# A gated attention, pooling and ConvFFN layer on one core: first q weights on ScalarE's queue, k's heads copied ahead of pooled tiles, the second norm's squares on ScalarE and its sums inside the first up tiles

## The chip, the core and the metric

The kernel runs on one core of one Trainium2 chip. The metric is the device time of one execution in microseconds (us). Three timed executions of the kernel before are given, and one further execution was profiled. Engines are named as in the profile: PE is TensorE's matmul (PEld its weight load), DVE is VectorE, ACT is ScalarE, POOL is GpSimd, SP is SyncE, and a name with q behind it (SPq) is that engine's instruction issue.

## The reference

One decoder layer over 256 tokens of width 1024, in float32:

```python
h = rmsnorm(x, norm_mix_g)
q, k, v, u_pool, gate_logits = split(h @ w_in)         # 512, 512, 512, 512, 2048
q, k = rotary(rmsnorm(heads(q))), rotary(rmsnorm(heads(k)))
attn = causal_softmax_attention(q, k, heads(v))        # 8 heads of 64; one block of 256, so plain causal
pooled = multiscale_pool_mixer(u_pool, w_pool, pool_scale)
gates = sigmoid(gate_logits + b_gate)
x = x + (gates[0] * (attn @ w_branch_attn) + gates[1] * (pooled @ w_branch_pool)) @ w_out
h2 = rmsnorm(x, norm_ffn_g)
gate, val = split(causal_depthwise_conv(h2 @ w_up, conv_w, conv_b))   # 2 x 2816 columns
return x + (silu(gate) * val) @ w_down
```

## The kernel before, in words

Everything is kept transposed, features on the 128 partitions and the 256 tokens along the free axis. Each float32 operand is split into a rounded high part (`high`, line 80, a copy on ACT) and a rest (`low`, lines 84 and 86, a subtraction on DVE), and `mm3` (lines 92 to 94) adds three matmuls: high by high, high by low, low by high. So each weight chunk of 1 MB (128 x 2048) needs two ACT copies (`hi_...`) and two DVE subtractions (`lo_...`) of 128 x 1024 before PE may use it. The calls of `ahead()` that are strewn through the program emit these pieces some chunks before their use, and the subtraction that ends a chunk lets SP issue the next weight transfer (`load`).

The stages follow each other: the start (x and q's weights come interleaved in the tensor `xq` by five transfers on SP's queue, lines 191 to 195, of 1, 1, 2, 2 and 2 of the eight contraction slices; eight small matmuls on `ones`, `ps_warm`, run on PE in the meantime); projections q, k, v (`project`, `ps_q`, `ps_k`, `ps_v`); four pool tiles (`ps_u`) and sixteen gate tiles (`ps_g`, the loop of line 497), among which attention is woven; the two branches (`ps_bp`, `ps_ba`); the output projection (`ps_out`, eight tiles, each followed by `residual`); then 44 up tiles (`ps_up`) and 22 down steps (`ps_d`); at the end eight output transfers on SP's queue (line 700).

The order on every engine is the order in which the program is written, and each engine runs its instructions in that order. The parts that the change touches:

- Line 189 is a first tiny activation on ACT, which makes ACT load its function table. Line 194 issues the `xq` transfers.
- `to_heads` (line 310) transposes a normed q or k tile on PE into a PSUM bank (`ps_tq`, `ps_tk`) and copies it on ACT to `qkT`. For k it is called at the head of iteration n = 1 (`KREADY`), behind what `tick()` and `ahead()` of iteration 0 put on ACT: a copy of a pooled tile (`poolh`, line 400) and a high part (`hi_g`). `scores` (line 426) at n = 2 multiplies q and k (`ps_s`).
- `residual` (line 566) runs once per output tile j: DVE adds the tile to x (`xq`, line 567), ACT makes the high part of the scaled x (`hhi`), POOL squares x (`ss`, `s`, lines 571 and 574) and adds the square to the sum `ss2` (line 575), `ahead()` puts an ACT copy and a DVE subtraction of a weight piece in between, and DVE makes the rest (`hlo`, line 577).
- `token_rms` (line 235) sums `ss2` over the partitions by two tiny matmuls (`ps_n`, line 238), DVE scales the result (`var_n`, line 240), POOL takes it to the power -0.5 (`rtok`, line 241). `diagonal` (line 243) puts `rtok` on a diagonal on DVE (`diag`), `spread_rms` (line 247) spreads it over all partitions by a matmul (`ps_n`, line 249) and copies it to `R2`. Every up tile is multiplied by `R2` when it leaves PSUM (line 606).
- Lines 649 to 664 are the first up tiles: both tiles of chunk 0 over seven of eight contraction slices, then their last slice, then the sums, then six slices of the next tile, then the spread.

Of the kernel before, what the change touches and what calls it, by code (L numbers as in the profile page):

```python
# [10 lines left out]
AF = mybir.ActivationFunctionType  # L11
ALU = mybir.AluOpType
AX = mybir.AxisListType

P = 128
S = 256
NT = S // P
# [36 lines left out]
KREADY = 1  # L54
# [5 lines left out]
def hybrid_layer_kernel(ctx: ExitStack, tc: tile.TileContext, xq_d, par_d, wkv_d, wpg_d,  # L60
# [128 lines left out]
    nc.scalar.activation(scrap, ones[:, 0:1], AF.Copy)  # L189

    cut = 0
    for k in XCUTS:
        end = KD + k * (S + AW)
        nc.sync.dma_start(out=xq_all[:, cut:end], in_=xq_d[:, cut:end])
        cut = end
    load(2)
# [300 lines left out]
    for n in range(2 * KD):  # L497
        if n == KREADY:
            for t in range(NT):
                to_heads(kg[t], t, kT, "k")  # L500
        if n >= FIRST and (n - FIRST) % 4 == 0:
            scores((n - FIRST) // 4)
        if n == 10:
            pool_maps()
            ahead()
        b, c = n // 2, n % 2
        if c == 0:
            w = chunk("g")
        ps = feature_tile(w, c, f"g{n}")
        tick()  # L510
        ahead(AHEAD if n % 2 else 0)
        nc.vector.tensor_tensor(gate(n), ps[:, 0:S], R1, ALU.mult)
        if n >= 2 * KD - 2:
            sigmoids(3)
# [51 lines left out]
    def residual(j, ps):  # L566
        nc.vector.tensor_tensor(xT[:, j, :], ps[:, 0:S], xT[:, j, :], ALU.add)
        g = par[:, C_FFN + j:C_FFN + j + 1]
        high(hhi[:, j, :], xT[:, j, :], g)
        if j == 0:  # L570
            nc.gpsimd.tensor_tensor(ss2, xT[:, j, :], xT[:, j, :], ALU.mult)
        else:
            s2 = tmp.tile([P, S], F32, tag="s2", name=f"s2_{j}")
            nc.gpsimd.tensor_tensor(s2, xT[:, j, :], xT[:, j, :], ALU.mult)
            nc.gpsimd.tensor_tensor(ss2, ss2, s2, ALU.add)
        ahead(AHEAD if j % 2 == 0 else 0)
        low(hlo[:, j, :], hhi[:, j, :], xT[:, j, :], g)
# [73 lines left out]
    for ks in (range(KD - 1), range(KD - 1, KD)):  # L651
        for c in range(2):
            tile_part(w0, (hhi, hlo), c, ps0[c], ks)
    ahead()
    ahead()
    stat = ps2.tile([P, 2, 512], F32, tag="ps2", name="ps_n2")
    token_rms(stat[:, 0, :], ss2, rtok2, "n2")
    ahead()
    w = chunk("up")
    ps = [bank("ps_up1_0")]  # L660
    tile_part(w, (hhi, hlo), 0, ps[0], range(6))
    diagonal(rtok2)
    spread_rms(stat[:, 1, 0:S], R2)
    tile_part(w, (hhi, hlo), 0, ps[0], range(6, KD))
# [30 lines left out]
    for m in (0, 2, 4, 6, 1, 3, 5, 7):  # L695
# [4 lines left out]
        nc.sync.dma_start(out=out_d[:, m, :], in_=xT[:, m, :])  # L700
# [73 lines left out]
```

## Time and profile before

| what | us |
|---|---|
| median of three timed executions | 350.35 |
| the three | 350.35, 350.55, 348.51 |
| the profiled execution, whole | 348.69 |
| its span | 346.9 |
| PE busy in the span | 340.7 (98%) |
| DVE, ACT, POOL busy | 261.0, 195.7, 101.5 |

The span is the stretch that the profiler shows, from the first instruction to the last; the profiled execution is 1.8 us longer than its span. PE's busy time counts pipelined matmuls with modelled ends: two matmuls that follow each other at full pace overlap in the records, so a stall of PE is read from the distance between starts, not from gaps of the busy time. A row of the timeline has start, duration, engine, line, operation, output and inputs, shapes, count, and in brackets how long the engine was idle before and who ended that.

### The profile page before, as it was taken

To read this page: it belongs to the slowest core of one execution; us is meant where nothing else is said; L and a number is where in the kernel's file an instruction comes from. 1 tells how busy PE (TensorE), PEld (TensorE's weight loads), DVE (VectorE), ACT (ScalarE), POOL (GpSimd) and SP (SyncE) were. 2 spreads that over 40 slices of the span, in tenths; PEclk is the share of its full clock that TensorE was granted. 3 is DMA by queue.
4 is the path that set the end of the run, shared out by engine and by line. 5 is a ranking of instruction groups with operands and counts; after the bars stand their busy time and mean duration, and the time that the engine had idled before them with its cause. 6 is when DMAs were issued, how large, how long until landed. Compare 5 with 4: busy or idle time off the path is not lost.

```text
span 346.9 us, 6715 instructions
## 1 busy us (share of the span) xinstructions
PE 340.7 (98%) x2736; PEld 329.2 (95%) x2736; DVE 261.0 (75%) x411; ACT 195.7 (56%) x311; POOL 101.5 (29%) x111
## 2 busy tenths in 40 slices
PE   8999999999999999999999999999999999999996
PEld 6887899999899999999999999999999999999995
DVE  4969889787587585899699877776777777777643
ACT  4956534634748945665367655555555555646420
POOL 1007991112202034586232212121212121212230
PEclk9999999999999999999999999999999999999999
DMA  7985642465272651566257555464636363652003
GB/s 275 419 327 213 222 159 110 150 220 213 69 259 92 242 201 45 175 237 211 109 168 271 188 224 201 164 222 145 242 123 243 131 235 132 232 162 83 0 2 121
DMA packets 10254, 62.76 MB, mean 181 GB/s; under 512 B 1136, under 2 KB 2288, under 8 KB 3312
## 3 DMA queue, kind: packets, MB, share of 16 engines
q1 hardware_dynamic: 10224, 62.34, 49.5%
q8 instruction: 21, 0.34, 0.4%
q14 instruction: 9, 0.07, 0.1%
HBM read 61.29 MB, written 1.05 MB: 180 GB/s over the span
## 4 chain that ended last, share of the span: by engine, by line
PE 80%; DVE 10%; DMA 4%; ACT 2%; issue 2%; SPq 1%; POOL 0%; ACTq 0%
PE ps_up L93 11%; PE ps_up L94 11%; PE ps_up L92 11%; PE ps_d L636 6%; PE ps_d L637 6%; PE ps_d L635 6%; PE ps_g L92 4%; PE ps_g L94 4%; PE ps_g L93 4%; DMA raw_k<-in_wkv 4%; PE ps_v L278 3%; DVE lo_up L84 2%; DVE hlo L86 2%; PE ps_bp L92 1%; PE ps_ba L94 1%
## 5 line engine op out<-in xcount | busy, mean ns | idle before, releaser
L92 PE MATMUL ps_up<-hhi,hi_up 128*128 128x256 f32 x352 | 98.5, 280 | 0.0
L93 PE MATMUL ps_up<-hlo,hi_up 128*128 128x256 f32 x352 | 98.4, 279 | 0.1
L94 PE MATMUL ps_up<-hhi,lo_up 128*128 128x256 f32 x352 | 98.3, 279 | 0.0
L93 PEld LDWEIGHTS ps_up<-hlo,hi_up 128*128 128x128 f32 x352 | 66.2, 188 | 0.4 <-DVE hlo L86 0.4
L92 PEld LDWEIGHTS ps_up<-hhi,hi_up 128*128 128x128 f32 x352 | 66.2, 188 | 0.0
L94 PEld LDWEIGHTS ps_up<-hhi,lo_up 128*128 128x128 f32 x352 | 66.2, 188 | 0.0
L84 DVE TENSOR_TENSOR lo_up<-raw_up,hi_up 128x1024 fp32r<-128x1024 f32 x44 | 55.9, 1273 | 6.1 <-ACT hi_up L80 6.1
L618 POOL TENSOR_TENSOR c_v<-c_g,c_v 128x256 f32<-128x256 f32 x22 | 16.2, 738 | 120.8 <-DVE c_v L601 120.8
L636 PE MATMUL ps_d<-al,hi_dn 128*128 128x256 f32 x176 | 49.1, 279 | 0.0
L635 PE MATMUL ps_d<-ah,hi_dn 128*128 128x256 f32 x176 | 49.1, 279 | 0.0
L637 PE MATMUL ps_d<-ah,lo_dn 128*128 128x256 f32 x176 | 49.1, 279 | 0.0
L80 ACT ACTIVATE hi_up<-raw_up 128x1024 fp32r<-128x1024 f32 x44 | 44.9, 1045 | 0.0
L92 PE MATMUL ps_g<-xhi,hi_g 128*128 128x256 f32 x128 | 36.5, 285 | 0.0
L93 PE MATMUL ps_g<-xlo,hi_g 128*128 128x256 f32 x128 | 35.7, 279 | 0.0
L94 PE MATMUL ps_g<-xhi,lo_g 128*128 128x256 f32 x128 | 35.7, 279 | 0.0
L80 ACT ACTIVATE ah<-c_v 128x256 fp32r<-128x256 f32 x22 | 9.2, 418 | 45.8 <-POOL c_v L618 45.8
L637 PEld LDWEIGHTS ps_d<-ah,lo_dn 128*128 128x128 f32 x176 | 33.1, 188 | 0.0
L635 PEld LDWEIGHTS ps_d<-ah,hi_dn 128*128 128x128 f32 x176 | 33.1, 188 | 0.0
L636 PEld LDWEIGHTS ps_d<-al,hi_dn 128*128 128x128 f32 x176 | 33.1, 188 | 0.0
L606 DVE TENSOR_TENSOR u_v<-ps_up,R 128x256 f32<-128x256 f32 x22 | 9.3, 421 | 26.1 <-PE ps_up L94 26.1
L84 DVE TENSOR_TENSOR lo_dn<-raw_dn,hi_dn 128x1024 fp32r<-128x1024 f32 x22 | 27.8, 1264 | 0.4 <-ACT hi_dn L80 0.4
L642 POOL TENSOR_TENSOR al<-c_v,ah 128x256 fp32r<-128x256 f32 x22 | 23.0, 1045 | 11.6 <-ACT ah L80 11.6
(182 smaller groups left out, 815.8 us busy)
## 6 DMA issues: line engine op xcount, KB each, us to landing
raw_up<-in_wup SPq DMA_DIRECT2D x22, 1024.0 KB, 4.8
raw_dn<-in_wdn SPq DMA_DIRECT2D x11, 1024.0 KB, 4.8
raw_g<-in_wpg SPq DMA_DIRECT2D x8, 1024.0 KB, 4.8
raw_o<-in_wout SPq DMA_DIRECT2D x4, 1024.0 KB, 4.8
xq<-in_xq SPq DMA_DIRECT2D x3, 768.0 KB, 7.4
raw_v<-in_wkv SPq DMA_DIRECT2D x2, 1024.0 KB, 14.1
raw_p<-in_wpg SPq DMA_DIRECT2D x2, 1024.0 KB, 6.3
raw_bp<-in_wbp SPq DMA_DIRECT2D x2, 1024.0 KB, 4.8
```

Source lines behind the costliest of these rows:

```text
L80: nc.scalar.activation(hi, src, AF.Copy, scale=scale)
L84: nc.vector.tensor_tensor(lo, src, hi.bitcast(F32), ALU.subtract)
L92: nc.tensor.matmul(out, sh, mh, start=start, stop=False, **kw)
L93: nc.tensor.matmul(out, sh, ml, start=False, stop=False, **kw)
L94: nc.tensor.matmul(out, sl, mh, start=False, stop=stop, **kw)
L278: nc.tensor.matmul(pt[t], sx[:, k, t * P:(t + 1) * P], wx[:, sl], start=k == 0 and sx is xhi and wx is hi, stop=k == KD - 1 and wx is lo)
L606: nc.vector.tensor_tensor(u, ps[:, 0:S], R2, ALU.mult)
L618: nc.gpsimd.tensor_tensor(uc[1], g[1], uc[1], ALU.mult)
L635: nc.tensor.matmul(o, hi[:, sl], acch[i], start=first, stop=False, skip_group_check=True)
L636: nc.tensor.matmul(o, hi[:, sl], accl[i], start=False, stop=False, skip_group_check=True)
L637: nc.tensor.matmul(o, lo[:, sl], acch[i], start=False, stop=i == KF - 1, skip_group_check=True)
L642: nc.gpsimd.tensor_tensor(accl[i], act_i, acch[i].bitcast(F32), ALU.subtract)
```

## The change

The transfer of the first slice is cut in two: its 512 columns of q weights are issued by ACT, its 264 columns of x (with the norm's gains) by SP, and the tiny activation that loads ACT's table goes behind the loop. `KREADY` becomes 0, and the call of `to_heads` for k stands behind the first gate tile and ahead of `tick()`. In `residual` the eight squares go from POOL to ACT; the seven additions stay on POOL. The sums of `token_rms` go ahead of the last slice of chunk 0's tiles, the three calls of `ahead()` behind that slice, and the spread behind all eight slices of the next tile. The last of the eight output transfers is cut into two halves of 64 partitions, one on SP's queue, one on ACT's.

```diff
--- before.py
+++ after.py
@@ -51,7 +51,7 @@
 STAGGER = 1
 AHEAD = 4
 FFN_AHEAD = 6
-KREADY = 1
+KREADY = 0
 FIRST = 2
 XCUTS = (1, 2, 4, 6, 8)
 
@@ -186,13 +186,18 @@
     xlo = act.tile([P, KD, S], F32R, tag="xlo", name="xlo")
     par = const.tile([P, C_END], F32, name="par")
     scrap = const.tile([P, 1], F32, name="scrap")
-    nc.scalar.activation(scrap, ones[:, 0:1], AF.Copy)
 
     cut = 0
     for k in XCUTS:
         end = KD + k * (S + AW)
-        nc.sync.dma_start(out=xq_all[:, cut:end], in_=xq_d[:, cut:end])
+        if k == 1:
+
+            nc.scalar.dma_start(out=xq_all[:, KD + S:end], in_=xq_d[:, KD + S:end])
+            nc.sync.dma_start(out=xq_all[:, 0:KD + S], in_=xq_d[:, 0:KD + S])
+        else:
+            nc.sync.dma_start(out=xq_all[:, cut:end], in_=xq_d[:, cut:end])
         cut = end
+    nc.scalar.activation(scrap, ones[:, 0:1], AF.Copy)
     load(2)
     nc.sync.dma_start(out=par, in_=par_d)
     for _ in range(RAWBUFS - 1):
@@ -495,9 +500,6 @@
             low(pooll[:, g, :], poolh[:, g, :], o, par[:, C_PS + g:C_PS + g + 1])
 
     for n in range(2 * KD):
-        if n == KREADY:
-            for t in range(NT):
-                to_heads(kg[t], t, kT, "k")
         if n >= FIRST and (n - FIRST) % 4 == 0:
             scores((n - FIRST) // 4)
         if n == 10:
@@ -507,6 +509,9 @@
         if c == 0:
             w = chunk("g")
         ps = feature_tile(w, c, f"g{n}")
+        if n == KREADY:
+            for t in range(NT):
+                to_heads(kg[t], t, kT, "k")
         tick()
         ahead(AHEAD if n % 2 else 0)
         nc.vector.tensor_tensor(gate(n), ps[:, 0:S], R1, ALU.mult)
@@ -568,10 +573,10 @@
         g = par[:, C_FFN + j:C_FFN + j + 1]
         high(hhi[:, j, :], xT[:, j, :], g)
         if j == 0:
-            nc.gpsimd.tensor_tensor(ss2, xT[:, j, :], xT[:, j, :], ALU.mult)
+            nc.scalar.activation(ss2, xT[:, j, :], AF.Square)
         else:
             s2 = tmp.tile([P, S], F32, tag="s2", name=f"s2_{j}")
-            nc.gpsimd.tensor_tensor(s2, xT[:, j, :], xT[:, j, :], ALU.mult)
+            nc.scalar.activation(s2, xT[:, j, :], AF.Square)
             nc.gpsimd.tensor_tensor(ss2, ss2, s2, ALU.add)
         ahead(AHEAD if j % 2 == 0 else 0)
         low(hlo[:, j, :], hhi[:, j, :], xT[:, j, :], g)
@@ -648,20 +653,19 @@
 
     w0 = chunk("up")
     ps0 = [bank(f"ps_up0_{c}") for c in range(2)]
-    for ks in (range(KD - 1), range(KD - 1, KD)):
-        for c in range(2):
-            tile_part(w0, (hhi, hlo), c, ps0[c], ks)
-    ahead()
-    ahead()
+    for c in range(2):
+        tile_part(w0, (hhi, hlo), c, ps0[c], range(KD - 1))
     stat = ps2.tile([P, 2, 512], F32, tag="ps2", name="ps_n2")
     token_rms(stat[:, 0, :], ss2, rtok2, "n2")
-    ahead()
+    for c in range(2):
+        tile_part(w0, (hhi, hlo), c, ps0[c], range(KD - 1, KD))
+    for _ in range(3):
+        ahead()
     w = chunk("up")
     ps = [bank("ps_up1_0")]
-    tile_part(w, (hhi, hlo), 0, ps[0], range(6))
+    tile_part(w, (hhi, hlo), 0, ps[0], range(KD))
     diagonal(rtok2)
     spread_rms(stat[:, 1, 0:S], R2)
-    tile_part(w, (hhi, hlo), 0, ps[0], range(6, KD))
     ug = normed(ps0[0], 0, "g0")
     uv = normed(ps0[1], KF, "v0")
     gate_done(0, ug)
@@ -697,7 +701,10 @@
             down(i, (m,))
         o = acc[m // 2][:, (m % 2) * S:(m % 2 + 1) * S]
         nc.vector.tensor_tensor(xT[:, m, :], o, xT[:, m, :], ALU.add)
-        nc.sync.dma_start(out=out_d[:, m, :], in_=xT[:, m, :])
+        if m < 7:
+            nc.sync.dma_start(out=out_d[:, m, :], in_=xT[:, m, :])
+    for q, rows in ((nc.sync, slice(0, P // 2)), (nc.scalar, slice(P // 2, P))):
+        q.dma_start(out=out_d[rows, 7, :], in_=xT[rows, 7, :])
 
 
     last = {}
```

Three places where instructions stand otherwise. The first is ACT around the copies of k's heads (`qkT<-ps_tk`); `poolh<-pl` are copies of pooled tiles, `hi_g` high parts of gate weights. Before:

```order
L80 ACTIVATE poolh<-pl_600 128x256
L80 ACTIVATE hi_g_560<-raw_g_363 128x1024
L80 ACTIVATE poolh<-pl_647 128x256
L80 ACTIVATE hi_g_654<-raw_g_427 128x1024
L315 ACTIVATE qkT<-ps_tk_661 128x4x128
L315 ACTIVATE qkT<-ps_tk_667 128x4x128
L80 ACTIVATE poolh<-pl_698 128x256
```

And in the changed kernel:

```order
L80 ACTIVATE poolh<-pl_601 128x256
L80 ACTIVATE hi_g_561<-raw_g_364 128x1024
L320 ACTIVATE qkT<-ps_tk_648 128x4x128
L320 ACTIVATE qkT<-ps_tk_654 128x4x128
L80 ACTIVATE poolh<-pl_660 128x256
L80 ACTIVATE hi_g_667<-raw_g_428 128x1024
L80 ACTIVATE poolh<-pl_699 128x256
```

The two copies of k's heads have moved ahead of one pooled tile and one high part; PE's order does not change there.

The second place is PE in the first up tiles. `ps_up_0` and `ps_up_1` are the two tiles of chunk 0 (high part `hi_up_1713` before, `hi_up_1714` after), the third tile uses the next chunk, and `ps_n` are the sums. Before:

```order
L94 MATMUL ps_up_1_1893<-hhi,lo_up_1714 128x256
L92 MATMUL ps_up_0_1892<-hhi,hi_up_1713 128x256
L93 MATMUL ps_up_0_1892<-hlo,hi_up_1713 128x256
L94 MATMUL ps_up_0_1892<-hhi,lo_up_1714 128x256
L92 MATMUL ps_up_1_1893<-hhi,hi_up_1713 128x256
L93 MATMUL ps_up_1_1893<-hlo,hi_up_1713 128x256
L94 MATMUL ps_up_1_1893<-hhi,lo_up_1714 128x256
L238 MATMUL ps_n_1950<-ones,ss_1604 128x1 x2
L92 MATMUL ps_up_0_1956<-hhi,hi_up_1783 128x256
```

And in the changed kernel:

```order
L94 MATMUL ps_up_1_1894<-hhi,lo_up_1715 128x256
L243 MATMUL ps_n_1937<-ones,ss_1605 128x1 x2
L92 MATMUL ps_up_0_1893<-hhi,hi_up_1714 128x256
L93 MATMUL ps_up_0_1893<-hlo,hi_up_1714 128x256
L94 MATMUL ps_up_0_1893<-hhi,lo_up_1715 128x256
L92 MATMUL ps_up_1_1894<-hhi,hi_up_1714 128x256
L93 MATMUL ps_up_1_1894<-hlo,hi_up_1714 128x256
L94 MATMUL ps_up_1_1894<-hhi,lo_up_1715 128x256
L92 MATMUL ps_up_0_1957<-hhi,hi_up_1784 128x256
```

The sums have moved ahead of six matmuls. The spread stands 18 matmuls into the third tile before, and behind all 24 of it after.

The third place is DVE behind the last residual. `lo_up` of two numbers are pieces of two later chunks. Before:

```order
L86 SCALAR_TENSOR_TENSOR hlo<-xq,par,hhi 128x256
L84 TENSOR_TENSOR lo_up_1854<-raw_up_1677,hi_up_1853 128x1024
L84 TENSOR_TENSOR lo_up_1943<-raw_up_1717,hi_up_1942 128x1024
L240 TENSOR_SCALAR var_n_1953<-ps_n_1950 128x2
L245 TENSOR_SCALAR diag<-ident,rtok_165 128x128 x2
L250 COPY R_164<-ps_n_1950 128x256
```

And in the changed kernel:

```order
L86 SCALAR_TENSOR_TENSOR hlo<-xq,par,hhi 128x256
L245 TENSOR_SCALAR var_n_1940<-ps_n_1937 128x2
L84 TENSOR_TENSOR lo_up_1855<-raw_up_1678,hi_up_1854 128x1024
L84 TENSOR_TENSOR lo_up_1950<-raw_up_1718,hi_up_1949 128x1024
L250 TENSOR_SCALAR diag<-ident,rtok_166 128x128 x2
L255 COPY R_165<-ps_n_1937 128x256
```

`var_n` has moved ahead of two subtractions of 128 x 1024, which stand between it and `diag` now.

## Rows read from the trace of the kernel before

**Rows 1.** The page: busy time, share of the span and instructions of each engine; and the shares of the engines in the chain of work that ended last.
```profile
PE 340.7 (98%) x2736; PEld 329.2 (95%) x2736; DVE 261.0 (75%) x411; ACT 195.7 (56%) x311; POOL 101.5 (29%) x111
...
PE 80%; DVE 10%; DMA 4%; ACT 2%; issue 2%; SPq 1%; POOL 0%; ACTq 0%
```

**Rows 2.** The list of waits, three of PE's weight loads that the prediction speaks of: engine, tile and line that waited, what ended the wait, us in total, times, longest.
```profile
PEld ps_s L430 <- ACT qkT L315: 0.7, 1, 0.7
...
PEld ps_n L249 <- DVE diag L245: 0.6, 1, 0.6
...
PEld ps_up L93 <- DVE hlo L86: 0.4, 1, 0.4
```

**Rows 3.** The busy time of each engine in the stretch of the up and down stage: from and to, length, then for PE, PEld, DVE, ACT and POOL busy us and instructions, granted clock, DMA share, GB/s.
```profile
166.00:344.00 178.00, 177.62 (x1520) 177.37 (x1520) 130.74 (x200) 97.16 (x146) 39.22 (x44) 1.00 0.45 162
```

**Rows 4.** The timeline of the scores' place, ACT first, then PE.
```profile
53.90 1.04 ACT L80 ACTIVATE hi_g<-raw_g 128x1024 fp32r<-128x1024 f32 x1
57.88 0.42 ACT L80 ACTIVATE poolh<-pl 128x256 fp32r<-128x256 f32 x1 [2.94 <-DVE pl L399]
...
59.15 1.06 ACT L315 ACTIVATE qkT<-ps_tk 128x512 f32<-128x512 f32 x2
```
```profile
55.96 1.04 PE L314 MATMUL ps_tk<-ident,qg_k 128*128 128x128 f32 x8
...
59.52 0.27 PE L94 MATMUL ps_g<-xhi,lo_g 128*128 128x256 f32 x1
60.27 0.71 PE L430 MATMUL ps_s<-qkT 64*128 64x256 f32 x4 [0.47 <-ACT qkT L315]
```

**Rows 5.** The timeline of the second norm, PE alone.
```profile
158.76 0.28 PE L92 MATMUL ps_up<-hhi,hi_up 128*128 128x256 f32 x1
...
159.19 0.39 PE L93 MATMUL ps_up<-hlo,hi_up 128*128 128x256 f32 x1
...
162.69 0.50 PE L238 MATMUL ps_n<-ones,ss 128*128 128x1 f32 x4
163.05 0.36 PE L92 MATMUL ps_up<-hhi,hi_up 128*128 128x256 f32 x1
...
165.12 0.28 PE L94 MATMUL ps_up<-hhi,lo_up 128*128 128x256 f32 x1
165.82 0.70 PE L249 MATMUL ps_n<-diag,ones 128*128 128x256 f32 x2 [0.42 <-DVE diag L245]
```

**Rows 6.** The same stage on DVE: a wait for a high part at the first residual, then the last residual and what follows it.
```profile
141.66 1.23 DVE L84 TENSOR_TENSOR lo_o<-raw_o,hi_o 128x1024 fp32r<-128x1024 f32 x1 [0.39 <-ACT hi_o L80]
...
156.62 0.41 DVE L567 TENSOR_TENSOR xq<-ps_out,xq 128x256 f32<-128x256 f32 x1
...
159.06 0.41 DVE L567 TENSOR_TENSOR xq<-ps_out,xq 128x256 f32<-128x256 f32 x1
159.39 1.42 DVE L84 TENSOR_TENSOR lo_up<-raw_up,hi_up 128x1024 fp32r<-128x1024 f32 x1
160.74 0.83 DVE L86 SCALAR_TENSOR_TENSOR hlo<-xq,par,hhi 128x256 fp32r<-128x256 f32 x1
161.50 2.90 DVE L84 TENSOR_TENSOR lo_up<-raw_up,hi_up 128x1024 fp32r<-128x1024 f32 x2
164.32 0.15 DVE L240 TENSOR_SCALAR var_n<-ps_n 128x2 f32<-128x2 f32 x1
165.29 0.48 DVE L245 TENSOR_SCALAR diag<-ident,rtok 128x128 f32<-128x128 f32 x2 [0.82 <-POOL rtok L241]
```

**Rows 7.** The same stage on POOL, and the durations of the rests on DVE's line 86 (ns, least, median, most): the first norm's (`xlo`, while POOL is idle) and the second norm's (`hlo`).
```profile
159.70 1.59 POOL L574 TENSOR_TENSOR s<-xq 128x256 f32<-128x256 f32 x1
161.37 0.81 POOL L575 TENSOR_TENSOR ss<-ss,s 128x256 f32<-128x256 f32 x1
```
```profile
L86 DVE SCALAR_TENSOR_TENSOR xlo<-xq,xhi x8: 478/480/485, 4.8 to 13.3; 128x256 fp32r<-128x256 f32 x8
L86 DVE SCALAR_TENSOR_TENSOR hlo<-xq,par,hhi x8: 476/831/952, 142.8 to 160.7; 128x256 fp32r<-128x256 f32 x8
```

**Rows 8.** The timeline of the start.
```profile
0.74 2.40 SPq L194 DMA_DIRECT2D xq<-in_xq  x5
...
4.43 0.63 ACT L80 ACTIVATE hi_q<-xq 128x512 fp32r<-128x512 f32 x1 [2.20 <-DMA xq<-in_xq]
...
5.11 1.12 PE L278 MATMUL ps_q<-hi_q,xhi 128*128 128x512 f32 x2 [0.28 <-ACT hi_q L80]
...
7.65 0.51 ACT L80 ACTIVATE xhi<-xq 128x256 fp32r<-128x256 f32 x1 [0.87 <-DMA xq<-in_xq]
...
7.93 0.63 PE L278 MATMUL ps_q<-lo_q,xhi 128*128 128x512 f32 x2
...
8.73 0.74 PE L278 MATMUL ps_q<-hi_q,xhi 128*128 128x512 f32 x2 [0.17 <-ACT hi_q L80]
```

**Rows 9.** The list of DMA issues: tile and source, queue, count, KB each, us from issue to landing.
```profile
out_T<-xq SPq DMA_DIRECT2D x8, 128.0 KB, 1.9
xq<-in_xq SPq DMA_DIRECT2D x1, 388.0 KB, 3.7
...
raw_pool<-in_wpool SPq DMA_DIRECT2D x1, 256.0 KB, 2.6
```

**Rows 10.** The output transfers by their tile: durations of the issues in ns (least, median, most), first and last start.
```profile
L700 SPq DMA_DIRECT2D out_T<-xq x8: 332/332/348, 339.2 to 344.1; - x8
```

## The prediction

> **What bounds the kernel now.** I read the page first: PE is busy for 340.7 of 346.9 us, the others 75% and less, and 80% of the chain that ended last is PE, 10% DVE [rows 1]. So a change can win only where PE stands still. Then the pace: 1520 matmuls in the 178.00 us from 166 to 344, so 0.117 us from one start to the next, without a stall over all that stretch [rows 3]. About half of the kernel, and all that follows the second norm, is therefore fixed, and I looked for stalls only before it. The list of waits names three that the change aims at: scores on the copy of k's heads, up matmuls on `hlo`, the spread on `diag` [rows 2]. Their price I take from starts, less one pace: 60.27 - 59.52 - 0.117 = 0.63 us [rows 4]; 159.19 - 158.76 - 0.117 = 0.31 us and 165.82 - 165.12 - 0.117 = 0.58 us [rows 5]. Sum 1.52 us. The other two places, start and end, are no waits on an engine but on transfers.
>
> **Scores.** The transposes of k's heads end at 57.0 on PE, but ACT copies only from 59.15, behind a pooled tile that came late from DVE and a high part. ACT stood idle for 2.94 us before that pooled tile, from 54.94 to 57.88 [rows 4]. In the new order the copies find that hole: from about 57.0, two copies in 1.06 us, done by 58.1, while PE arrives at the scores at 59.64. The whole 0.63 us goes. The pooled tile, ready at 57.88, slips by 0.2 us, and the high part behind it too, which PE needs only some tiles later. Nothing is issued more or less. What is late next? From here PE's order is the same, and gate tiles need pieces that were made a chunk ahead; the list of waits has no further one of PE or its weight loads from there to the up tiles of over 0.3 us, so I carry the 0.63 us through, with 0.3 as the low end.
>
> **Squares from POOL to ACT.** POOL loses eight squares, of 1.59 us for the last [rows 7], and keeps seven additions of 0.81. ACT gains eight squares of 128 x 256. This kernel has none of that shape; the copy of a pooled tile of that shape takes 0.42 us [rows 4], so 8 x 0.42 = 3.4 us on ACT, some 0.33 each in a row. ACT waits for DVE in that stage, except that the first residual's subtraction waits already 0.39 us for its high part [rows 6]: there the square delays DVE by 0.33 us, and once more at the third residual, where two pieces are due again: 0.66 us against the change.
>
> For it speaks DVE's relief. DVE runs behind PE here: one residual takes 159.06 - 156.62 = 2.44 us, of which a subtraction of 1.42 and an `hlo` of 0.83 [rows 6], which without POOL beside it takes 0.48 [rows 7]. The last square began at 159.70 and ended at 161.29, across the end of the subtraction and the start of `hlo` at 160.74 [rows 6, 7]. After the change the addition stands there instead: ready about 1.3 us after the residual, so again at the end of the subtraction. So I leave `hlo` at 0.83 and give back only the subtraction's excess over a free one (1.23 in the first row of rows 6): 0.2 us a residual. Over six residuals 1.2 us, less the 0.66, leaves 0.5 us, and the wait for `hlo` needs 0.31. It goes, narrowly: credit 0.31, bounds 0 (the lag stays) and 0.31; below nothing in a rival.
>
> The Trainium skill ("SBUF — State Buffer", Who interferes with whom) says that VectorE with two SBUF inputs and GpSimd take turns on one shared port pair, whole instruction by whole instruction, the second one blocked until the first is through. The trace agrees that both are slowed, but 0.35 us of `hlo` is less than a whole POOL operation of 0.81. By the rule taken literally `hlo` would wait for a full addition; that is rival 3.
>
> **Sums earlier.** Call the start of the sums t. Before, PE goes on at t + 0.36, and `var_n` at 164.32 is held by two subtractions in front of it on DVE, so `diag` starts at 165.29 and PE stalls [rows 5, 6]. After, `var_n` runs when the sums are there, about t + 0.55 (0.50 for the sums [rows 5] and a little for the signal), POOL's power runs beside the two subtractions (2.90 us for the pair before, 2.3 to 2.9 now), and `diag` (0.48) ends between t + 3.5 and t + 4.1. PE reaches the spread at t + 0.36 + 30 x 0.117 = t + 3.87: six matmuls and a whole tile of 24. So the stall of 0.58 us falls to between 0 and 0.25; I take 0. The price is that DVE waits at `var_n` for PE: behind it stand the two subtractions and the load they release, for chunks that PE starts over 5 us later, which covers it. The sums themselves need the last addition: before, at 162.18 [rows 7]; now they are due at 156.66 + 42 x 0.117 = 161.6. With the square on ACT and no DVE lag the addition ends near 160; with the old lag it would end at 161.3 at the latest. `R` comes 0.3 us later relative to the tile, and a PSUM bank is needed only a tile (2.8 us) later: cost nothing.
>
> **Start.** The first matmul at 5.11 follows the landing at 4.43 and one ACT copy. But PE stands again before 8.73: 8.73 - 7.93 - 2 x 0.233 = 0.33 us (two matmuls of twice the columns, so of two paces each), since the third slice's transfer (x's `xhi` at 7.65 waited for it) is late [rows 8]. So a first matmul earlier by any amount gains nothing unless the third transfer is earlier as well, and one later by 0.33 us costs nothing. The bytes ahead of the third are the same. The issue on ACT (0.48 us, a fifth of SP's 2.40) and the table load behind it fall into ACT's 2.20 us of idleness. I take 0; bounds: a gain of 0.33 if both queues ramp up faster, a loss of 6.2 if q's weights land with the last of SP's `xq` transfers.
>
> **End.** The last transfer of 128 KB lands 1.9 us after its issue; 256 KB took 2.6, so half the size would be 0.35 us shorter if halves ran apart [rows 9]. Issues are 0.33 us each, on two queues side by side [rows 10]. I take 0, since the two halves together are the same bytes, and keep 0.35 gained to 0.1 lost as the range.
>
> The Trainium skill ("DMA: Bandwidth & Descriptors", Rules for kernel authors) speaks against both edits: two transfers to partition halves serialize on the same 16 engines, and issuing from several queues only saves issue time. All transfers here left from SP, so no row shows it. By the rule the end gains 0, without it 0.35.
>
> **Sum.** 0.63 + 0.31 + 0.58 = 1.52 us. The profiled execution of 348.69 would become 347.2. The three timed runs lie at 348.51 and around 350.45, so the profiled one belongs to their lower end; off the median, 350.35 - 1.5 = 348.8.
>
> **The rivals.** (1) Start or end give as well: 0.33 at the third slice and 0.35 at the end, sum 2.2 us: 348.1. For it: the first transfer of 388 KB took 3.7 us where 256 KB took 2.6 [rows 9]. Against: the same bytes. 14 in 100. (2) The stalls in the norm move instead of going: squares hold up ACT's high parts, DVE stays behind, PE waits as long for `hlo` or `diag`. Only 0.63 stays: 349.7. For it: the margins of 0.2 to 0.4 us above are thin. 15 in 100. (3) POOL's addition, now always ready as the subtraction ends, blocks `hlo` for its full 0.81 instead of 0.35: a residual takes 2.24 + 0.46 = 2.70 us, 0.26 more than before, over five residuals 1.3, with ACT's 0.66 some 2.0 late, in place of the 0.31: 0.63 + 0.58 - 1.7 = -0.5: 350.8. Against: PE's tile takes 2.8 us, so DVE would still keep up. 6 in 100. (4) The slower one: q's weights on ACT's queue share the engines with four transfers of SP and land with the third slice, at 7.65 instead of 4.43. PE starts 3.2 us later, 0.33 of it free: +2.9, net +1.4: 351.7. It decides from a landing at 4.43 + 0.33 + 1.52 = 6.3. Against: at equal shares they land when twice their bytes have moved, near 4.4. 5 in 100. The forecast has the remaining 60.
>
> **How the numbers follow.** The likeliest case is 348.8, by itself 346.9 (if the lower of the two groups of times is met, 348.51 - 1.52 = 347.0) to 349.4. The range reaches to 350.8 (rivals 2 and 3, and the upper group) and to 346.4 (rival 1 in the lower group). About 1% is what a measurement of this kernel tells from no change. Faster by over 1% means under 346.85: the forecast in the lowest runs (8 in 100) and half of rival 1 (7). Slower by over 1% means over 353.9: only rival 4 near its far end, 4 in 100. The rest, 81, lies within 1%.
>
> **What would show it.** Right: scores follow the gate tile at one pace, with ACT's copies near 57; no wait for `hlo`, and start distances of 0.117 through the first up tiles; `var_n` ahead of its subtractions, and a spread with under 0.25 us of stall; first matmul anywhere up to 5.4 with the one near 8.73 unmoved; the last transfer landing 1.9 us after its issue. Wrong: the wait for `hlo` longer than 0.4 us, `hlo` over 1.2 us, a first matmul after 5.5, or new stalls between 61 and 139 that eat the 0.63.

## The result, and the profile after

The changed kernel takes 347.80 us (median of 13 runs, 347.71 to 348.66), the kernel before 350.14 (13 runs, 348.40 to 350.59): a ratio of 0.9949, 95% interval 0.9934 to 0.9964. The forecast was 348.8 in a range of 346.4 to 350.8, so the time lies inside it and within 1% of before. The executions of both kernels fall into a lower and an upper group (before: 6 of 13 at 348.40 to 348.81, 7 at 350.14 to 350.59; after: 11 at 347.71 to 348.01, 2 at 348.5 to 348.7); what five profiled executions show of this stands in the last section, and where the text compares tenths it takes the lower group. Like for like the change is worth 0.9 us: the profiled executions have spans of 346.9 and 346.0, and the lower groups have medians of 348.6 and 347.8. Three single executions in the experiments took 560 to 1866 us; they count in the medians of runs 1, 4 and 7 and are in no ratio and no group.

The page: busy time and instructions of each engine, and the engines' shares of the chain that ended last.
```profile
PE 340.3 (98%) x2736; PEld 329.3 (95%) x2736; DVE 259.3 (75%) x411; ACT 198.1 (57%) x319; POOL 89.4 (26%) x103
...
PE 90%; DMA 5%; DVE 3%; ACT 1%; issue 0%; POOL 0%; SPq 0%; ACTq 0%
```
Eight squares have gone from POOL to ACT, and DVE's share of the chain has fallen from 10% to 3% [rows 1]: PE waits for DVE much less. The list of waits has one of a weight load that was not there before (engine, tile and line that waited, what ended the wait, us, times, longest):
```profile
PEld ps_up L94 <- DVE lo_up L84: 0.2, 1, 0.2
```
The three waits of [rows 2] are gone from the list.

**Scores.** The timeline of their place, ACT, then PE:
```profile
56.51 1.09 ACT L320 ACTIVATE qkT<-ps_tk 128x512 f32<-128x512 f32 x2 [1.65 <-PE ps_tk L319]
57.79 0.42 ACT L80 ACTIVATE poolh<-pl 128x256 fp32r<-128x256 f32 x1 [0.19 <-DVE pl L404]
```
```profile
59.44 0.27 PE L94 MATMUL ps_g<-xhi,lo_g 128*128 128x256 f32 x1
59.64 0.71 PE L435 MATMUL ps_s<-qkT 64*128 64x256 f32 x4
```
The copies stand in the hole ahead of the pooled tile and end at 57.6, and PE goes on without a wait. From the last gate matmul to the first of the scores it is 59.64 - 59.44 = 0.20 us, where [rows 4] have 60.27 - 59.52 = 0.75: the place became 0.55 us shorter. PE is here 0.08 us earlier already (59.44 against 59.52).

**Second norm.** PE, DVE and POOL, in that order:
```profile
160.94 0.50 PE L243 MATMUL ps_n<-ones,ss 128*128 128x1 f32 x4
...
164.77 0.28 PE L94 MATMUL ps_up<-hhi,lo_up 128*128 128x256 f32 x1
164.88 0.59 PE L254 MATMUL ps_n<-diag,ones 128*128 128x256 f32 x2
...
183.65 0.28 PE L93 MATMUL ps_up<-hlo,hi_up 128*128 128x256 f32 x1
183.95 0.39 PE L94 MATMUL ps_up<-hhi,lo_up 128*128 128x256 f32 x1
184.18 0.28 PE L92 MATMUL ps_up<-hhi,hi_up 128*128 128x256 f32 x1
```
```profile
141.35 1.22 DVE L84 TENSOR_TENSOR lo_o<-raw_o,hi_o 128x1024 fp32r<-128x1024 f32 x1 [0.70 <-ACT hi_o L80]
...
144.35 0.48 DVE L86 SCALAR_TENSOR_TENSOR hlo<-xq,par,hhi 128x256 fp32r<-128x256 f32 x1
...
155.61 0.41 DVE L572 TENSOR_TENSOR xq<-ps_out,xq 128x256 f32<-128x256 f32 x1
...
157.96 0.41 DVE L572 TENSOR_TENSOR xq<-ps_out,xq 128x256 f32<-128x256 f32 x1
158.29 1.21 DVE L84 TENSOR_TENSOR lo_up<-raw_up,hi_up 128x1024 fp32r<-128x1024 f32 x1
159.42 0.97 DVE L86 SCALAR_TENSOR_TENSOR hlo<-xq,par,hhi 128x256 fp32r<-128x256 f32 x1
161.47 0.16 DVE L245 TENSOR_SCALAR var_n<-ps_n 128x2 f32<-128x2 f32 x1 [1.08 <-PE ps_n L243]
161.55 2.35 DVE L84 TENSOR_TENSOR lo_up<-raw_up,hi_up 128x1024 fp32r<-128x1024 f32 x2
163.82 0.48 DVE L250 TENSOR_SCALAR diag<-ident,rtok 128x128 f32<-128x128 f32 x2
165.52 0.42 DVE L255 COPY R<-ps_n 128x256 f32<-128x256 f32 x1 [1.22 <-PE ps_n L254]
```
```profile
159.36 0.75 POOL L580 TENSOR_TENSOR ss<-ss,s 128x256 f32<-128x256 f32 x1 [1.61 <-ACT s L579]
161.71 1.62 POOL L246 TENSOR_TENSOR rtok<-var_n,mhalf 128x2 f32<-128x2 f32 x1 [1.60 <-DVE var_n L245]
```
PE no longer waits for `hlo`, and the spread follows its predecessor by one pace of 0.11 us; in [rows 5] it came 0.70 after. The last residuals take DVE 157.96 - 155.61 = 2.35 us each instead of 2.44 [rows 6]: the subtraction fell from 1.42 to 1.21, `hlo` rose from 0.83 to 0.97. But PE waits at 183.95 for a `lo_up`: 183.95 - 183.65 - 0.12 = 0.18, and the matmul behind it starts 0.23 later instead of 0.12, so this stop costs 0.29 us in all. The stop at `hlo` in the kernel before had the same form; this row follows the one at 159.19 in [rows 5]:
```profile
159.42 0.28 PE L94 MATMUL ps_up<-hhi,lo_up 128*128 128x256 f32 x1
```

**Start and end.** The timeline of the start:
```profile
0.74 0.39 SPq L196 DMA_DIRECT2D xq<-in_xq  x1
0.74 0.41 ACTq L195 DMA_DIRECT2D xq<-in_xq  x1
...
5.27 1.22 PE L283 MATMUL ps_q<-hi_q,xhi 128*128 128x512 f32 x2 [0.43 <-DVE xlo L86]
...
7.63 0.51 ACT L80 ACTIVATE xhi<-xq 128x256 fp32r<-128x256 f32 x1 [0.81 <-DMA xq<-in_xq]
```
The first matmul comes at 5.27 instead of 5.11; the third slice's copy is where it was, at 7.63 against 7.65 [rows 8]. The end, the issues of the two halves first, then their rows in the list of DMA issues (count, KB each, us from the start of the issue to landing):
```profile
342.68 0.55 SPq L707 DMA_DIRECT2D out_T<-xq  x1
342.68 0.56 ACTq L707 DMA_DIRECT2D out_T<-xq  x1
```
```profile
out_T<-xq SPq DMA_DIRECT2D x1, 64.0 KB, 2.2
out_T<-xq ACTq DMA_DIRECT2D x1, 64.0 KB, 2.5
```
Each half takes 0.55 us to issue, where a whole tile took 0.33 [rows 10], and 2.2 and 2.5 us to land, where a whole tile took 1.9 [rows 9]. The span ends 346.0 - 342.68 = 3.3 us after the start of the last issue; before it was 346.9 - 344.1 = 2.8.

**The ledger of the two spans**, from starts on PE. To the first up matmul: 156.66 before, 156.04 after, 0.62 gained, of which 0.08 is there ahead of the scores already. From there through the spread to the next steady matmul: 166.48 - 156.66 = 9.82 against 165.44 - 156.04 = 9.40, and since the spread now stands 6 matmuls (0.70 us) later, 8.70 like for like: 1.12 gained. From there to the last matmul: 343.35 - 166.48 = 176.87 against 341.91 - 165.44 + 0.70 = 177.17: 0.30 lost, which is the stop at 183.95. The end: 346.9 - 343.35 = 3.55 against 346.0 - 341.91 = 4.09, 0.54 lost. Together 0.62 + 1.12 - 0.30 - 0.54 = 0.90, which is the difference of the spans.

### The profile page after: what moved, and what is told of

Same layout as the page of the kernel before. It is cut to its first block, busy times and chain, and to the rows that moved or that the text cites. A ratio compares the mean times of both kernels' runs of the same rounds, so it can differ in the third digit from the quotient of the medians.

```text
span 346.0 us, 6726 instructions
## 1 busy us (share of the span) xinstructions
PE 340.3 (98%) x2736; PEld 329.3 (95%) x2736; DVE 259.3 (75%) x411; ACT 198.1 (57%) x319; POOL 89.4 (26%) x103
## 3 DMA queue, kind: packets, MB, share of 16 engines
HBM read 61.29 MB, written 1.05 MB: 180 GB/s over the span
## 4 chain that ended last, share of the span: by engine, by line
PE 90%; DMA 5%; DVE 3%; ACT 1%; issue 0%; POOL 0%; SPq 0%; ACTq 0%
PE ps_up L94 12%; PE ps_up L92 12%; PE ps_up L93 12%; PE ps_d L642 6%; PE ps_d L641 6%; PE ps_d L640 6%; PE ps_g L92 5%; PE ps_g L94 4%; PE ps_g L93 4%; DMA raw_k<-in_wkv 3%; PE ps_v L283 3%; PE ps_out L92 2%; PE ps_out L94 2%; PE ps_out L93 2%; PE ps_bp L92 1%; DMA xq<-in_xq 1%
## 5 line engine op out<-in xcount | busy, mean ns | idle before, releaser
L84 DVE TENSOR_TENSOR lo_up<-raw_up,hi_up 128x1024 fp32r<-128x1024 f32 x44 | 54.5, 1242 | 6.1 <-ACT hi_up L80 6.1
```

What stands on the lines that cost most here:

```text
L84: nc.vector.tensor_tensor(lo, src, hi.bitcast(F32), ALU.subtract)
```

## The experiments

The medians of the kernel before beside these runs were 348.71, 348.77 and 348.81 (32 to 35 runs each, lower group around 348.65). "Lower" is the median of a kernel's lower group, with the number of executions in it.

**1. The end undone.** The changed kernel with the last tile as one transfer on SP.
```diff
-        if m < 7:
-            nc.sync.dma_start(out=out_d[:, m, :], in_=xT[:, m, :])
-    for q, rows in ((nc.sync, slice(0, P // 2)), (nc.scalar, slice(P // 2, P))):
-        q.dma_start(out=out_d[rows, 7, :], in_=xT[rows, 7, :])
+        nc.sync.dma_start(out=out_d[:, m, :], in_=xT[:, m, :])
```


> The changed kernel with its last output transfer whole again, on SP's queue, so the end edit alone undone. In the changed kernel's trace the two halves took 0.55 us to issue side by side and landed 2.2 and 2.5 us after, where the whole took 0.33 and 1.9; PE ends its last matmul 1.42 us earlier than before, but the span is only 0.9 us shorter. Theory A (the end edit costs what the issue and the landing grew by): the time from the last issue to the span's end falls by about 0.5 us, and the time from 347.8 to about 347.2 to 347.3. Rival B (the end of the span is set by something else, the closing instructions): span and time stay within 0.15 us of the changed kernel, 347.7 to 347.9.

Measured: 347.22 median, ratio to before 0.9944 (0.9923 to 0.9964); lower 347.16 (6 of 8), against the changed kernel's 347.79 (11 of 13). That is theory A: the end of the change costs 0.6 us. This is the best version by its median, ahead of both kernels.

**2. The norm alone.** Before, with the squares on ACT and the sums inside the first up tiles.
```diff
-            nc.gpsimd.tensor_tensor(s2, xT[:, j, :], xT[:, j, :], ALU.mult)
+            nc.scalar.activation(s2, xT[:, j, :], AF.Square)
...
-    tile_part(w, (hhi, hlo), 0, ps[0], range(6))
+    tile_part(w, (hhi, hlo), 0, ps[0], range(KD))
     diagonal(rtok2)
     spread_rms(stat[:, 1, 0:S], R2)
-    tile_part(w, (hhi, hlo), 0, ps[0], range(6, KD))
```


> The kernel before with the second norm's edits alone (squares on ScalarE, sums inside the first up tiles, spread after the whole tile). Theory A (stalls add up): the waits on hlo and diag go, 0.31 + 0.58 = 0.89 us, the span is about 346.0 and the runs near the lower group of before (348.5) become 347.6. Rival B (the gain needs the scores' edit as well, or is given back in the up tiles): under 0.4 us. On the two groups of before's times (near 348.5 and near 350.3): theory C says the upper group comes from this stage, where DVE and POOL take turns; then no run of this kernel lies over 349. Otherwise about half of the runs still lie 1.7 us above the others, near 349.4.

Measured: 347.89 median, ratio 0.9972 (0.9954 to 0.9990); lower 347.79 (8 of 12). That is 0.86 under before's lower group, 0.2 short of theory A. The waits for `hlo` and `diag` are gone, that of the scores (0.6) is there, and the one for `lo_up` (0.3) has come: it belongs to the norm's edits. The sign of theory C, no execution over 349, did not come: three lie at 349.2 to 349.5.

**3. The scores alone.**
```diff
-KREADY = 1
+KREADY = 0
...
         ps = feature_tile(w, c, f"g{n}")
+        if n == KREADY:
+            for t in range(NT):
+                to_heads(kg[t], t, kT, "k")
```


> The kernel before with k's heads copied ahead of the pooled tile alone. Theory A: the scores' stall of 0.63 us goes and is not given back: the span is about 346.3, runs of the lower group near 347.9. Rival B (taken back before the up tiles): under 0.2 us, 348.4. On the groups of times: if the upper group has its cause at the scores, no run over 349; otherwise about half of the runs are near 349.7.

Measured: 348.03 median, ratio 0.9968 (0.9948 to 0.9988); lower 348.02 (10 of 12), 0.63 under before. The wait of the scores is gone, those for `hlo` and `diag` stand as they were (0.4 and 0.6 in the list of waits). Theory A holds: the gain at the scores arrives at the end. Two executions are near 349.7, so the upper group stays without the scores' wait.

**4. The start alone.**
```diff
-        nc.sync.dma_start(out=xq_all[:, cut:end], in_=xq_d[:, cut:end])
+        if k == 1:
+            nc.scalar.dma_start(out=xq_all[:, KD + S:end], in_=xq_d[:, KD + S:end])
+            nc.sync.dma_start(out=xq_all[:, 0:KD + S], in_=xq_d[:, 0:KD + S])
+        else:
+            nc.sync.dma_start(out=xq_all[:, cut:end], in_=xq_d[:, cut:end])
```


> The kernel before with the first q weights on ScalarE's queue alone. Theory A (the bytes are the same): the first matmul comes at 5.2 to 5.4, the third slice's wait hides that, and the time is within 0.15 us of before like for like: 348.4 to 348.6 in the lower group. Rival B (the two queues ramp up faster): up to 0.3 us less. On the groups of times: if the upper group comes from how the first transfers land, no run over 349; otherwise about half of the runs are near 350.3, as before.

Measured: 348.60 median, ratio 0.9977 (0.9957 to 0.9998); lower 348.56 (11 of 12): nothing, within 0.1. The first matmul for k comes at 17.02 to 17.33 in the eight traces with this edit (mean 17.17) and at 17.07 to 17.34 in the six without (mean 17.20). The profiled execution was the one of the upper group (350.24), so that group stays with the other start. Up to the up tiles this execution has the waits of the kernel before, and no wait after them, yet its last matmul starts 1.6 us later. That opened the question of the pace, below.

**5 and 6. What the end's loss is made of.** Both halves on SP's queue; and one whole transfer on ACT's queue.
```diff
-    for q, rows in ((nc.sync, slice(0, P // 2)), (nc.scalar, slice(P // 2, P))):
+    for q, rows in ((nc.sync, slice(0, P // 2)), (nc.sync, slice(P // 2, P))):
```


> The changed kernel, with both halves of the last output tile issued on SP's queue (none on ScalarE's). The changed kernel is at 347.80 us and its twin with one whole transfer at 347.1 to 347.2. Theory A (a transfer of 64 partitions is no quicker than one of 128, whichever queue carries it, and the second issue comes on top): 347.8 to 348.0, both halves landing in 2.2 us or more. Theory B (the loss is ScalarE's queue: an issue of 0.56 us and a landing of 2.5 us, and two issues at the same moment): 347.2 to 347.5, issues back at 0.33 us.

```diff
-        if m < 7:
-            nc.sync.dma_start(out=out_d[:, m, :], in_=xT[:, m, :])
-    for q, rows in ((nc.sync, slice(0, P // 2)), (nc.scalar, slice(P // 2, P))):
-        q.dma_start(out=out_d[rows, 7, :], in_=xT[rows, 7, :])
+        (nc.sync if m < 7 else nc.scalar).dma_start(out=out_d[:, m, :], in_=xT[:, m, :])
```


> The changed kernel, with the last output tile as one whole transfer of 128 KB, on ScalarE's queue instead of SP's. Theory A (the loss is in cutting the tile in two): 347.1 to 347.3, a landing of 1.9 to 2.0 us. Theory B (the loss is ScalarE's queue): 347.6 to 347.9, an issue of 0.55 us and a landing near 2.5 us.

Measured: halves on SP 348.25, ratio 0.9974 (0.9954 to 0.9995), lower 348.21 (8 of 12). Whole on ACT 347.32, ratio 0.9958 (0.9935 to 0.9980), lower 347.23 (7 of 12). The list of DMA issues, of the halves on SP, then of the whole tile on ACT:
```profile
out_T<-xq SPq DMA_DIRECT2D x2, 64.0 KB, 2.2
```
```profile
out_T<-xq ACTq DMA_DIRECT2D x1, 128.0 KB, 1.9
```
Theory A is shown, though the halves on SP came 0.2 above its range: ACT's queue is as good as SP's to within 0.1, and it is the cut that costs. The two halves on SP take 1.17 us to issue, one after the other, and the kernel is 1.05 us slower than with the whole transfer of run 1; with the halves on two queues it is 0.63.

**7. Cut by columns instead.**
```diff
-    for q, rows in ((nc.sync, slice(0, P // 2)), (nc.scalar, slice(P // 2, P))):
-        q.dma_start(out=out_d[rows, 7, :], in_=xT[rows, 7, :])
+    for q, cols in ((nc.sync, slice(0, S // 2)), (nc.scalar, slice(S // 2, S))):
+        q.dma_start(out=out_d[:, 7, cols], in_=xT[:, 7, cols])
```


> The changed kernel, with the last output tile cut by columns (128 partitions x 128 columns to each of the two queues) instead of by partitions (64 x 256). The changed kernel is at 347.80, its twin with one whole transfer at 347.15 to 347.2. Theory A (a transfer of 64 partitions is slow to issue, 0.55 us, and to land): issues back to 0.33 to 0.36, 347.1 to 347.3. Theory B (two transfers at once, or twice the number of completions, cost it, whatever the cut): 347.7 to 347.9.

Measured: 347.61, ratio 0.9977 (0.9959 to 0.9994), lower 347.56 (7 of 11), the profiled one 347.27.
```profile
342.59 0.33 SPq L707 DMA_DIRECT2D out_T<-xq  x1
342.59 0.37 ACTq L707 DMA_DIRECT2D out_T<-xq  x1
```
```profile
out_T<-xq SPq DMA_DIRECT2D x1, 64.0 KB, 1.9
out_T<-xq ACTq DMA_DIRECT2D x1, 64.0 KB, 2.0
```
Issue and landing are those of a whole tile: the halves of the change are slow because they are cut by partitions, to 64 each. Yet the time lies between the two theories, 0.4 over one transfer in most runs and 0.1 in the profiled one; a second transfer seems to cost something by itself, which this run doesn't settle. In no form does a cut gain anything.

**8. The sums alone**, the squares left on POOL; the spread stands behind the whole third tile, as in the change.
```diff
-    for ks in (range(KD - 1), range(KD - 1, KD)):
-        for c in range(2):
-            tile_part(w0, (hhi, hlo), c, ps0[c], ks)
+    for c in range(2):
+        tile_part(w0, (hhi, hlo), c, ps0[c], range(KD - 1))
...
     token_rms(stat[:, 0, :], ss2, rtok2, "n2")
+    for c in range(2):
+        tile_part(w0, (hhi, hlo), c, ps0[c], range(KD - 1, KD))
```


> The kernel before, with the second norm's sums moved into the first up tiles and nothing else: the squares stay on GpSimd. Theory A (the two edits of the norm need each other): the sums now stand on TensorE where GpSimd's last addition, which ended at 162.18 in the kernel before, has not come: a stall of 0.6 to 1.0 us at ps_n takes the place of the hlo wait of 0.31 and of part of the 0.58 before the spread; 348.6 to 349.1 against 348.65, no gain. Rival B (each edit takes away its own stall): the spread's 0.58 goes and hlo's 0.31 stays, 348.1.

Measured: 348.60, ratio 0.9979 (0.9960 to 0.9999), lower 348.57 (10 of 12): 0.1 under before. The waits of the weight loads from 150 on:
```profile
PEld ps_up L93 <- DVE hlo L86: 0.4, 1, 0.4
PEld ps_n L238 <- POOL ss L575: 0.3, 1, 0.3
PEld ps_up L94 <- DVE lo_up L84: 0.3, 1, 0.3
```
That is theory A on the time, with two misses in the detail: the wait for `hlo` stayed whole, and the one at `ps_n` is 0.3 instead of 0.6 to 1.0. The spread's wait is gone, but POOL's last addition and, later, a `lo_up` take its place: to the steady matmul behind the spread the run is 0.35 faster like for like, and from there to the last matmul 0.32 slower.

**9. The squares alone**, the sums left where they were.
```diff
-            nc.gpsimd.tensor_tensor(s2, xT[:, j, :], xT[:, j, :], ALU.mult)
+            nc.scalar.activation(s2, xT[:, j, :], AF.Square)
```


> The kernel before, with the second norm's squares on ScalarE and nothing else: the sums stay where they were in TensorE's order. Theory A: VectorE's pieces come every 2.35 us instead of 2.43, so hlo's 0.31 goes, and the two subtractions ahead of var_n end about a microsecond earlier (163.3 instead of 164.3), so that most of the spread's 0.58 goes as well: 347.8 to 348.1 against 348.65. Rival B (each edit takes away its own stall): the spread's 0.58 stays, 348.35.

Measured: 349.18 median, ratio 0.9970 (0.9948 to 0.9992); lower 347.48 (5 of 12, 347.40 to 347.60), seven at 349.15 to 349.37. The profiled execution is of the lower group (347.41): DVE, then PE:
```profile
160.76 2.35 DVE L84 TENSOR_TENSOR lo_up<-raw_up,hi_up 128x1024 fp32r<-128x1024 f32 x2
163.03 0.15 DVE L240 TENSOR_SCALAR var_n<-ps_n 128x2 f32<-128x2 f32 x1
163.99 0.48 DVE L245 TENSOR_SCALAR diag<-ident,rtok 128x128 f32<-128x128 f32 x2 [0.82 <-POOL rtok L241]
165.28 0.42 DVE L250 COPY R<-ps_n 128x256 f32<-128x256 f32 x1 [0.80 <-PE ps_n L249]
...
182.47 1.22 DVE L84 TENSOR_TENSOR lo_up<-raw_up,hi_up 128x1024 fp32r<-128x1024 f32 x1
```
```profile
164.53 0.28 PE L94 MATMUL ps_up<-hhi,lo_up 128*128 128x256 f32 x1
164.65 0.59 PE L249 MATMUL ps_n<-diag,ones 128*128 128x256 f32 x2
```
Theory A holds, with more of it than expected: both waits of the norm are gone with the squares alone. DVE reaches `var_n` at 163.03 instead of 164.32 [rows 6], and `diag` is ready when PE comes. From 150 on no weight load waits for anything, the `lo_up` at 184 included. From the first up matmul (156.50 here) to the steady one behind the spread it is 8.69 us, 1.13 less than before: all that the two edits together gained.

So the other edit, moving the sums, has nothing left to win, and with the spread's later place it costs 0.3. The same DVE rows of run 2, whose first up matmul is at 156.63:
```profile
166.12 0.42 DVE L250 COPY R<-ps_n 128x256 f32<-128x256 f32 x1 [1.23 <-PE ps_n L249]
...
183.30 1.22 DVE L84 TENSOR_TENSOR lo_up<-raw_up,hi_up 128x1024 fp32r<-128x1024 f32 x1
```
The spread stands 6 matmuls later, so `R` comes 9.49 us behind the first up matmul instead of 8.78. All of DVE's gate work behind it shifts by as much, and the `lo_up` that PE needs at 184 with it (26.67 instead of 25.97). From the spread to the last matmul run 2 takes 0.3 us longer like for like, as the changed kernel does.

**10 and 11. Scores and squares alone; and with the start.** The edits are those of runs 3 and 9, and of run 4 besides; in short:
```diff
-KREADY = 1
+KREADY = 0
...
-            nc.gpsimd.tensor_tensor(s2, xT[:, j, :], xT[:, j, :], ALU.mult)
+            nc.scalar.activation(s2, xT[:, j, :], AF.Square)
```


> The kernel before, with two parts of the change alone: k's heads copied ahead of the pooled tiles, and the second norm's squares on ScalarE. The start, the place of the sums and the end stay as before. Theory A (the parts add, and moving the sums costs 0.4 once the squares are on ScalarE): 347.45 with the squares alone less the 0.62 of the scores, 346.8, ahead of both kernels. Theory B (the sums' move is needed, and the 347.4 with the squares alone came from elsewhere): 347.2 to 347.3, as with scores, squares and sums.

> As the run with the scores and the squares alone, and the change of the start besides (x on SP's queue, the first q weights on ScalarE's); sums and end as before. Theory A (the start is worth nothing, as predicted): within 0.15 of that run, 346.7 to 346.9. Rival B (it gains its third of a microsecond): 346.5. Rival C (its first matmul comes 0.16 later, and nothing after makes up for it): 346.95.

Measured: without the start 347.90, ratio 0.9963 (0.9943 to 0.9984), lower 347.13 (6 of 12), six at 348.60 to 349.03. With the start 348.75, ratio 0.9985 (0.9965 to 1.0005), one run at 346.86, one at 347.83, nine at 348.56 and above. Run 10 missed A by 0.3 and lies at B's edge; run 11 reached A's 346.9, but once. By the traces the norm is worth 1.13 and the scores 0.55, which would give 348.65 - 1.68 = 346.97; the rest, near 0.15, is within what the start varies from trace to trace (17.02 to 17.34, run 4). That neither beats run 1 by its median has another reason: most of their executions, the two profiled ones among them, are in the upper group.

**12. The spread moved back, the sums left moved.** Run 1 with
```diff
-    tile_part(w, (hhi, hlo), 0, ps[0], range(KD))
+    tile_part(w, (hhi, hlo), 0, ps[0], range(6))
     diagonal(rtok2)
     spread_rms(stat[:, 1, 0:S], R2)
+    tile_part(w, (hhi, hlo), 0, ps[0], range(6, KD))
```


> The changed kernel with the last output tile as one transfer on SP's queue, as the run at 347.15 to 347.2, and with the spread of the second norm's factor put back inside the third up tile, 6 of its 24 matmuls earlier; the sums stay moved. Theory A (the late spread delays VectorE's up work, and lo_up comes late for TensorE at 184): TensorE waits up to 0.2 at the spread, the factor is there 0.5 earlier, and the stall of 0.2 to 0.3 at 184 goes: 346.9 to 347.1. Theory B (the stall at 184 has another cause): 347.2 to 347.4, the stall at the spread on top.

Measured: 348.41, ratio 0.9970 (0.9948 to 0.9992), lower 347.28 (5 of 12). Its trace, of the upper group, has no wait at 184, as A says, but one at the spread, which waits for `diag` and starts 0.27 behind its predecessor:
```profile
164.23 0.70 PE L254 MATMUL ps_n<-diag,ones 128*128 128x256 f32 x2
```
The stage from the first up matmul to the steady one behind the spread is 0.27 longer, like for like, than in run 1, so this stop takes back the 0.30 of the one at 184. That fits the lower group's time, which is B's; no execution of the lower group was profiled. The trace bears out the cause of the stop at 184: `R` ends 9.47 us behind the first up matmul and the `lo_up` starts at 26.23, where run 9 has 9.20 and 25.97, run 2 9.91 and 26.67. In all three it follows `R` by 16.8 us, whether the sums are moved or not.

## Why the forecast was right, and where it was not

**The waits.** All three waits that were credited are gone, but none has the size of the forecast. The scores' 0.63 had one pace of 0.117 taken off the distance of 0.75; without a wait the distance is 0.20, so 0.55 was there to win. Run 3's 0.63 contains what the start varies. The norm gave 1.12 instead of 0.89, because a stop also delays the matmul behind it, which the forecast did not count: by 0.11 at `hlo` (159.42) and by 0.10 at the spread (0.35 from its start to the next up matmul instead of 0.25). With that, 0.31 becomes 0.42 and 0.58 becomes 0.68.

**Why the wait for `hlo` went.** DVE needs 21.30 us for the stage from the first residual to the end of the last `hlo` instead of 21.86: 0.56 gained, where the forecast had 1.2 - 0.66 = 0.5. The two waits for a high part did grow by 0.31 each, from 0.39 [rows 6] to 0.70 and from 0.18 to 0.49. The relief was made of other parts than forecast. The subtraction lost its 0.2, but the second and third `hlo` fell from 0.83 and 0.95 to 0.48, and the last five rose from 0.83 to 0.97, with POOL's addition beside them (159.36 to 160.11 beside the last, which starts at 159.42). That the sum came out so well is luck. The second `hlo` before:
```profile
144.67 0.83 DVE L86 SCALAR_TENSOR_TENSOR hlo<-xq,par,hhi 128x256 fp32r<-128x256 f32 x1
```
By the Trainium skill ("SBUF — State Buffer", Who interferes with whom) one of the two would stand until the other is through: 160.11 plus a free rest of 0.48 [rows 7] is 160.59. The trace agrees that `hlo` is held up, but not for so long: it ended at 160.39. Rival 3 had taken the blocking for a full addition on top of 0.48, which is 1.29; 0.97 was measured.

**Which edit did it.** The forecast gave 0.31 to the squares and 0.58 to the sums. Run 9 takes both waits away with the squares alone, and run 8 wins 0.1 with the sums and the later spread alone. The step that failed is the one that has `var_n` "held by two subtractions in front of it on DVE" and cures it by the new order: the subtractions end 1.3 us earlier anyway (163.11 instead of 164.40) once POOL's squares are gone, and that is enough. The new order even makes `diag` later: DVE stands 1.08 us at `var_n` for PE and has both subtractions behind it, so `diag` starts 163.82 - 156.04 = 7.78 us behind the first up matmul, in run 9 163.99 - 156.50 = 7.49. With the spread left early, that is the stop of run 12, where the stage to the steady matmul takes 8.97 us against 8.69 in run 9. The sums' move with the early spread and the squares on POOL was not run.

**"Cost nothing" for a later `R`.** The forecast looked at the PSUM bank alone. A later `R` means later gate work on DVE and a `lo_up` that is late at 184: 0.30 us, a term that the sum lacked.

**The end.** "I take 0", with 0.1 lost as the worst: 0.6 was lost (run 1). The two halves were costed by their bytes; what counted was the cut by partitions: each half takes 0.55 us to issue and lands 0.3 to 0.6 later than a whole tile, counted from the start of its issue (runs 5 to 7). The Trainium skill ("DMA: Bandwidth & Descriptors", Rules for kernel authors) advised against such halves since they serialize; the trace agrees on the advice and goes beyond it, a loss where serializing alone would give 0.

**The start.** 0 was forecast and 0 measured (run 4). The first matmul comes at 5.03 to 5.32 in the fourteen traces.

**The number.** The sum of 1.52 for the profiled execution should read 0.62 + 1.12 - 0.30 - 0.54 = 0.90. It was then taken off a median that lay in before's upper group, while 11 of 13 runs of the changed kernel are in its lower one: that is why the median came 1.0 under 348.8 although the change did 0.6 less than the sum. The range was met partly by luck, since these two errors have opposite signs.

## What to carry to other kernels

Price a wait by the distance that its place has without it, and count the matmul behind it too. Take that price into the sum once: of two edits aimed at neighbouring stalls, try each alone, since the first may leave the second only its side effects. Follow a factor that is moved later to all the work that hangs on it, not only to its first reader. Don't cut a small last transfer by partitions.

## What the runs showed of the hardware

TensorE has two steady paces at one granted clock, 1.00 (the level of 2.4 GHz). The stretches 72 to 152 and 190 to 330 of run 9 (lower group), then of run 10 (upper group); from and to, length, then busy us and instructions of PE, PEld, DVE, ACT, POOL, granted clock, DMA share, GB/s:
```profile
72.00:152.00 80.00, 79.90 (x682) 77.08 (x682) 58.18 (x95) 50.85 (x97) 16.59 (x17) 1.00 0.50 181
190.00:330.00 140.00, 140.00 (x1202) 140.00 (x1202) 102.81 (x152) 80.38 (x119) 29.95 (x34) 1.00 0.48 168
```
```profile
72.00:152.00 80.00, 79.90 (x682) 77.08 (x681) 58.59 (x95) 51.05 (x98) 16.60 (x17) 1.00 0.50 182
190.00:330.00 140.00, 140.00 (x1191) 140.00 (x1190) 101.40 (x151) 79.30 (x117) 29.55 (x33) 1.00 0.47 167
```
Up to 152 the counts agree; after 190 the upper group runs 1191 matmuls where the lower runs 1202, 0.9% fewer, with no wait in between and the same clock. By the starts it is 117.8 ns a matmul instead of 116.7, from one place on to the end: from the spread in the traces of runs 4, 10, 11 and 12, from the wait at 184 in that of run 6. Each time the pace changed at a place where TensorE's starts stand apart for a moment; the nine other traces pass the same places and keep the faster pace. Over the 1520 matmuls behind the spread that is 1.7 us, the distance of the two groups in most kernels. It does not explain all: some executions lie 0.7 to 1.0 above their lower group (both upper ones of the changed kernel do) and a few 2.4 to 3.3, and none of these was profiled.

The kernels with the squares on ACT whose spread stands early (runs 9 to 12) were above their lower group by 0.8 us and more in 30 of 47 executions, those with the later spread (after, runs 1, 2, 5, 6 and 7) by 0.7 and more in 21 of 68. So the sums' move, 0.3 slower by itself, may pay in the median by how often the slower pace is met. But the share is not steady: the kernel before was over 350 in 7 of 13 executions beside the result and in 9 of 32, 16 of 35 and 10 of 34 beside the experiments. What chooses the pace was not found; no edit here removed the upper group, and the shares are no proof of a cause.
